# A QKV product on one core: casts and turns of the first rows placed between products, and another order of the last pair's products and stores

## Chip, cores, metric

One core of one Trainium2 chip. The metric is the device time of one execution in microseconds (us). The kernel before had a median of 362.59 us in three runs (362.5 to 362.67) when the prediction was made.

## The reference

```python
# x: (16, 512, 768) float32, w_qkv: (768, 2304) float32
qkv = np.matmul(x, w_qkv)
q, k, v = qkv[..., :768], qkv[..., 768:1536], qkv[..., 1536:]
return np.stack([q, k, v], axis=0)
```

## The kernel before

PE is the matmul engine, DVE the vector engine, ACT the scalar engine, POOL GpSimd, SP the sync engine. The 8192 rows of x are worked in 32 pairs of 128-row blocks. The 2304 columns are four blocks of 512 and a remainder of 256. The first three pairs ("rows 1 to 6") are multiplied in bf16 directly; from the fourth pair on, each pair makes two quads a and b, of seven products each (named 1 to 7), with sums of x and of the weights prepared by POOL and DVE. A "turn" is a transpose on PE. The parts that matter:

```python
def copy_halves(dst, src, two):            # one half on DVE, the other on ACT
    nc.vector.tensor_copy(out=dst[0], in_=src[0])
    if two: nc.scalar.activation(dst[1], src[1], ident)
    else:   nc.vector.tensor_copy(out=dst[1], in_=src[1])
def cast_rows(p, two=True): ...            # both rows of pair p: xc (bf16) <- xin (fp32)
def turn_rows(p, two=True): ...            # per row: 6 transposes into PSUM, copy_halves to xb
def busy(n): ...                           # n matmuls on zeros, to get PE's clock up
# ... loads, in order: x pair 0, x pair 1, six k-blocks of weights, remainder weights, x pair 2, ...
busy(11)
cast_rows(0); turn_rows(0)
busy(4)
cast_rows(1); cast_k(0); cast_k(1)         # cast_k(j): k-block j of the weights to bf16, on DVE
turn_rows(1)
for j in range(2, KT): cast_k(j)
# ... casts of the remainder's weights
block(0, 0, b1[0], singles, nothing)       # rows 1 to 4, k by k: 24 products
rem(0); rem(1)                             # remainder columns of rows 1 to 4
cast_rows(2, False); turn_rows(2, False)
block(0, 0, b1[0], halves((4, 5)), nothing)     # rows 5 and 6: 12 products
# ... then the block with weights bt ("the products of bt"), two more blocks, and 29 pairs

def last(a, b):                            # the last pair
    do(a,1); do(b,1); do(a,2); do(a,6); do(b,2); do(b,6)
    for u in (a, b): store_cols(u, 0, 0, CB, nc.sync)
    for u in (a, b): do(u,5); do(u,7); store_cols(u, 1, CB, 2*CB, nc.sync)
    do(a,4); store_cols(a, 1, 0, CB, nc.scalar); rem_stored(0)
    do(b,4); store_cols(b, 1, 0, CB, nc.scalar)
    for u in (a, b): do(u,3); store_cols(u, 0, CB, 2*CB, nc.sync)
    rem_stored(1)
```

`rem_stored(r)` multiplies one row's remainder columns, copies them out of PSUM on ACT and issues their store on ACT. c21 is what product 4 makes, c12 what product 3 adds to.

## Time and profile before

| | value | how to read it |
|---|---|---|
| time | 362.59 us (362.5 to 362.67) | three timed runs |
| the profiled run | 363.13 us, span 361.3 us | the run from which the trace comes; note that it is 0.5 us slower than any of the three timed ones |
| PE busy | 98% | the middle is bound by the number of matmuls |
| turns of rows 3 and 4 start | 8.51 us | PE had waited for them; first product (matmul of x with weights) at 9.30 |
| first product of bt | 20.65 us | where everything that the change does at the head is over |
| PE ends | 356.96 us | about 4.4 us of stores and closing follow |

A transfer "lands" when the trace records its completion. The profile's lines that carry this are in the prediction below.

### The profile page before, as it was taken

What the parts mean: (1) busy time and instruction counts of PE and PEld (TensorE: products, weight loads), DVE (VectorE), ACT (ScalarE), POOL (GpSimd) and SP (SyncE); (2) the same over time, 40 slices, a digit from 0 to 9 for tenths busy, and PEclk for the clock granted to TensorE, in tenths of its full rate; (3) what the DMA queues carried; (4) which work ended last, traced back from release to release, by engine and by line L of the source; (5) the groups of instructions that cost most, each with busy time, mean ns of one, the idle gap of its engine ahead of it and who ended that gap; (6) DMA issues with size and microseconds to landing.
All of it is one profiled execution on the core that took longest, in us unless ns stands there. A gap on an engine that the chain in (4) does not pass through costs nothing.

```text
span 361.3 us, 5221 instructions
## 1 busy us (share of the span) xinstructions
PE 353.4 (98%) x1765; PEld 251.0 (69%) x1797; DVE 224.4 (62%) x239; ACT 182.9 (51%) x304; POOL 173.9 (48%) x180
## 2 busy tenths in 40 slices
PE   8999999999999999999999999999999999999995
PEld 3644577777777777777777777777777777777763
DVE  3499826765566765566675565676556676556642
ACT  4547555455454545454545445455545454545452
POOL 0001861746664445664445665444665444666410
PEclk9999999999999999999999999999999999999999
DMA  7999869988898999899899999998989899999666
GB/s 298 405 388 373 286 221 359 331 289 295 278 328 301 294 273 294 276 324 315 280 280 290 281 308 309 291 289 278 292 288 321 295 300 271 297 272 339 264 261 232
DMA packets 80617, 108.08 MB, mean 299 GB/s; under 512 B 4816, under 2 KB 60368, under 8 KB 80592
## 3 DMA queue, kind: packets, MB, share of 16 engines
q1 hardware_dynamic: 65184, 96.35, 80.8%
q10 hardware_dynamic: 15408, 11.41, 9.6%
q8 instruction: 14, 0.23, 0.3%
q14 instruction: 11, 0.09, 0.1%
HBM read 32.24 MB, written 75.50 MB: 298 GB/s over the span
## 4 chain that ended last, share of the span: by engine, by line
PE 96%; ACT 1%; issue 1%; ACTq 0%; DVE 0%
PE ps L212 75%; PE ps L262 11%; PE ps L385 9%; PE ps L365 1%; PE ps L167 1%; ACT o L243 0%; ACTq L303 0%; ACT xb L147 0%; ACT orem L317 0%; DVE xb L145 0%; ACT xc L147 0%; ACTq L319 0%; DVE zero L346 0%; ACTq L317 0%
## 5 line engine op out<-in xcount | busy, mean ns | idle before, releaser
L212 PE MATMUL ps<-t,s 128*128 128x512 f32 x696 | 173.8, 398 | 0.0
L212 PEld LDWEIGHTS ps<-t,s 128*128 128x128 f32 x696 | 130.7, 188 | 29.7
L175 POOL CAST xb<-xf 128x1536 bf16<-128x1536 f32 x29 | 43.8, 1510 | 168.3 <-DVE xf L130 156.0
L240 DVE TENSOR_TENSOR o<-o,ps 128x512 f32<-128x512 f32 x58 | 39.9, 688 | 91.2 <-ACT o L239 91.2
L130 DVE STREAM_TRANSPOSE xf<-xin 128x1536 f32<-128x1536 f32 x29 | 85.5, 2950 | 3.7 <-DMA out_dram<-orem 2.1
L212 PE MATMUL ps<-b,xb 128*128 128x512 bf16 x320 | 82.4, 380 | 1.5
L239 ACT ACTIVATE o<-ps 128x512 f32<-128x512 f32 x58 | 34.8, 600 | 44.2 <-PE ps L212 44.2
L212 PEld LDWEIGHTS <-xb 128*128 128x128 bf16 x348 | 31.7, 98 | 35.6 <-issue 7.3
L233 ACT ACTIVATE o<-ps 128x512 f32<-128x512 f32 x58 | 34.9, 601 | 42.1 <-PE ps L212 39.4
L246 DVE TENSOR_TENSOR o<-o,ps 128x512 f32<-128x512 f32 x58 | 39.9, 688 | 21.3 <-PE ps L212 20.2
L212 PE MATMUL ps<-b,s 128*128 128x512 f32 x174 | 48.7, 389 | 0.0
L262 PE MATMUL ps<-w_rem,xb 128*128 128x256 bf16 x384 | 47.2, 273 | 0.0
L243 ACT ACTIVATE o<-ps 128x512 f32<-128x512 f32 x58 | 34.7, 599 | 24.1 <-PE ps L212 21.3
L226 ACT ACTIVATE o<-ps 128x512 f32<-128x512 f32 x58 | 34.7, 598 | 23.8 <-DVE o L246 20.6
L262 PEld LDWEIGHTS <-xb 128*128 128x128 bf16 x384 | 37.4, 98 | 11.2 <-issue 0.5
L230 DVE TENSOR_TENSOR o<-o,ps 128x512 f32<-128x512 f32 x58 | 36.5, 673 | 5.4 <-PE ps L212 4.1
L212 PEld LDWEIGHTS ps<-b,s 128*128 128x128 f32 x174 | 32.7, 188 | 6.8
L184 POOL TENSOR_TENSOR s<-s,xf 128x384 fp32r<-128x384 f32 x29 | 30.0, 1035 | 2.3
L183 POOL TENSOR_TENSOR s<-xf 128x384 fp32r<-128x384 f32 x29 | 30.9, 1064 | 0.0
L185 POOL TENSOR_TENSOR s<-xf 128x384 fp32r<-128x384 f32 x29 | 29.5, 1017 | 0.0
L187 POOL TENSOR_TENSOR s<-xf,s 128x384 fp32r<-128x384 f32 x29 | 29.5, 1016 | 0.0
L272 ACT ACTIVATE orem<-ps 128x512 f32<-128x512 f32 x31 | 18.5, 598 | 20.7 <-PE ps L262 19.5
(36 smaller groups left out, 129.4 us busy)
## 6 DMA issues: line engine op xcount, KB each, us to landing
out_dram<-o SPq DMA_DIRECT2D x62, 768.0 KB, 4.8
out_dram<-o SPq DMA_DIRECT2D x65, 256.0 KB, 4.1
xin<-in_x_dram SPq DMA_DIRECT2D x62, 192.0 KB, 6.9
xin<-in_x_dram ACTq DMA_DIRECT2D x54, 192.0 KB, 4.4
out_dram<-orem SPq DMA_DIRECT2D x31, 256.0 KB, 5.7
st<-in_w_qkv_dram SPq DMA_DIRECT2D x6, 768.0 KB, 13.1
xin<-in_x_dram SPq DMA_DIRECT2D x3, 768.0 KB, 5.7
st<-in_w_qkv_dram SPq DMA_DIRECT2D x6, 256.0 KB, 6.1
```

The source lines that it names most:

```text
L130: nc.vector.transpose(t[:].rearrange("p j (g b) -> p g j b", b=G), xin.pop(p)[:].rearrange("p g (a j) -> p g j a", a=G),)
L175: nc.gpsimd.tensor_copy(out=xb[p][:], in_=xf[p][:])
L212: nc.tensor.matmul(ps[:], lhs[j], rhs[j], start=(start and j == 0), stop=(j == KH - 1), skip_group_check=True,)
L226: nc.scalar.activation(c11, u.x[:], ident)
L230: nc.vector.tensor_tensor(c11, c11, u.z[:], op=add)
L233: nc.scalar.activation(c12, u.x[:], ident)
L239: nc.scalar.activation(c22, u.x[:], ident)
L240: nc.vector.tensor_tensor(c22, c22, u.y[:], op=add)
L243: nc.scalar.activation(c21, u.x[:], ident)
L246: nc.vector.tensor_tensor(c12, c12, u.y[:], op=add)
L262: nc.tensor.matmul(ps, xb[p][:, j, r * P:(r + 1) * P], w_rem[j // KH][:, j % KH, :], start=(j == 0), stop=(j == KT - 1), skip_group_check= ...
L385: nc.tensor.matmul(ps[n][:], xb[p][:, j, r * P:(r + 1) * P], w[:, j, :], start=(j == 0), stop=(j == KT - 1), skip_group_check=True,)
```

## The change

Its intent: at the head, rows 3 and 4 are cast and turned one at a time, between the first products of rows 1 and 2; rows 5 and 6 are cast and turned one at a time, each behind one remainder. At the tail, the last pair's stores are spread so that fewer bytes are left at the end, and the last product's columns are added and stored in two halves. The core of the diff:

```diff
-    busy(4)
-    cast_rows(1)
-    cast_k(0)
-    cast_k(1)
-    turn_rows(1)
+    busy(4)
+    cast_row(1, 0)
+    cast_k(0)
+    cast_row(1, 1)
+    cast_k(1)
+    def third_row():
+        turn_row(1, 0)
+        cast_k(2)
+    def fourth_row():
+        turn_row(1, 1)
+        for j in range(3, KT): cast_k(j)
     ...
-    block(0, 0, b1[0], singles, nothing)
-    rem(0)
-    rem(1)
-    cast_rows(2, False)
-    turn_rows(2, False)
-    block(0, 0, b1[0], halves((4, 5)), nothing)
+    block(0, 0, b1[0],
+        [((0, ), (0, 1)), third_row, ((1, ), (0, 1)), fourth_row, ((0, 1), (2, 3))]
+        + [((j, ), range(4)) for j in range(2, KT)], nothing)
+    for p in range(2):
+        rem(p)
+        cast_row(2, p, False)
+        turn_row(2, p, False)
+    block(0, 0, b1[0], [(range(KT), (4, )), (range(KT), (5, ))], nothing)
     ... in last(a, b), after products 1 and 2 and the stores of c11:
+        do(a, 6); do(a, 5); do(b, 6); do(a, 7)
+        store_cols(a, 1, CB, 2 * CB, nc.sync)
+        do(b, 5); do(b, 7)
+        store_cols(b, 1, CB, 2 * CB, nc.sync)
+        do(a, 4)
+        store_cols(a, 1, 0, CB, nc.sync)
+        do(a, 3)
+        store_cols(a, 0, CB, 2 * CB, nc.sync)
+        rem_stored(0)
+        rem_stored(1)
+        do(b, 4)
+        store_cols(b, 1, 0, CB, nc.sync)
+        product(b, 3, b.y, False)
+        for lo in (CB, CB + CB // 2):
+            hi = lo + CB // 2
+            part = b.o[:, 0, lo:hi]
+            nc.vector.tensor_tensor(part, part, b.y[:, lo - CB:hi - CB], op=add)
+            store_cols(b, 0, lo, hi, nc.scalar)
```

The remainder's weights are also loaded in two transfers instead of one.

More of the change, by code (lines that the diff above doesn't have):

```diff
@@ L151, with cast_row, turn_row @@
     xc = {}
-    def cast_rows(p, two=True):
-        src = xin.pop(p)
-        xc[p] = s_pool.tile([P, 2, K], bf16, name="xc", tag="s")
-        for r in range(2):
-            halves = (slice(0, K // 2), slice(K // 2, K))
-            copy_halves([xc[p][:, r, n] for n in halves], [src[:, r, n] for n in halves], two)
-    def turn_rows(p, two=True):
-        c = xc.pop(p)
-        xb[p] = xb_pool.tile([P, KT, 2 * P], bf16, name="xb", tag="xb")
-        for r in range(2):
-            cols = c[:, r, :].rearrange("m (p j) -> m j p", j=KT)
-            ps = ps_pool.tile([P, KT, P], bf16, name="ps")
-            for j in range(KT):
-                nc.tensor.transpose(ps[:, j, :], cols[:, j, :], eye)
-            ks = (slice(0, KH), slice(KH, KT))
-            copy_halves(
-                [xb[p][:, n, r * P:(r + 1) * P] for n in ks], [ps[:, n, :] for n in ks], two
-            )
+    def cast_row(p, r, two=True):
+        if r == 0:
+            xc[p] = s_pool.tile([P, 2, K], bf16, name="xc", tag="s")
+        halves = (slice(0, K // 2), slice(K // 2, K))
+        copy_halves([xc[p][:, r, n] for n in halves], [xin[p][:, r, n] for n in halves], two)
+    def turn_row(p, r, two=True):
+        if r == 0:
+            xb[p] = xb_pool.tile([P, KT, 2 * P], bf16, name="xb", tag="xb")
+        cols = xc[p][:, r, :].rearrange("m (p j) -> m j p", j=KT)
+        ps = ps_pool.tile([P, KT, P], bf16, name="ps")
+        for j in range(KT):
+            nc.tensor.transpose(ps[:, j, :], cols[:, j, :], eye)
+        ks = (slice(0, KH), slice(KH, KT))
+        copy_halves(
+            [xb[p][:, n, r * P:(r + 1) * P] for n in ks], [ps[:, n, :] for n in ks], two
+        )
     def round_x(p):
@@ L319, in rem_stored @@
             nc.scalar.dma_start(out_flat[1, row:row + P, R_OFF - H:R_OFF - H + REM], o[:, 0, :])
-        do(a, 1)
-        do(b, 1)
-        do(a, 2)
-        do(a, 6)
-        do(b, 2)
-        do(b, 6)
+        for n in (1, 2):
+            for u in (a, b):
+                do(u, n)
         for u in (a, b):
             store_cols(u, 0, 0, CB, nc.sync)
-        for u in (a, b):
-            do(u, 5)
-            do(u, 7)
-            store_cols(u, 1, CB, 2 * CB, nc.sync)
+        do(a, 6)
+        do(a, 5)
+        do(b, 6)
+        do(a, 7)
+        store_cols(a, 1, CB, 2 * CB, nc.sync)
+        do(b, 5)
+        do(b, 7)
+        store_cols(b, 1, CB, 2 * CB, nc.sync)
         do(a, 4)
-        store_cols(a, 1, 0, CB, nc.scalar)
+        store_cols(a, 1, 0, CB, nc.sync)
+        do(a, 3)
+        store_cols(a, 0, CB, 2 * CB, nc.sync)
         rem_stored(0)
+        rem_stored(1)
         do(b, 4)
-        store_cols(b, 1, 0, CB, nc.scalar)
-        for u in (a, b):
-            do(u, 3)
-            store_cols(u, 0, CB, 2 * CB, nc.sync)
-        rem_stored(1)
+        store_cols(b, 1, 0, CB, nc.sync)
[5 more added lines that the diff above has]
+            store_cols(b, 0, lo, hi, nc.scalar)
     NS = 3
@@ L349, with load_k @@
     make_identity(nc, eye)
+    st_0 = tq_pool.tile([P, KT, CB], fp32, name="st0", tag="tq")
+    stage[0, 0, 0], stage[0, 1, 0] = st_0[:, :KH, :], st_0[:, KH:, :]
+    def load_k(j):
+        load_w(st_0[:, j:j + 1], j, 1, Q_OFF[0], CB)
     load_rows(1)
-    load_blocks(0, 0, 1)
+    for j in range(KT):
+        load_k(j)
     st_rem = o_pool.tile([P, KT, REM], fp32, name="str", tag="o")
-    load_w(st_rem[:], 0, KT, R_OFF, REM)
+    for h in range(2):
+        load_w(st_rem[:, h * KH:(h + 1) * KH], h * KH, KH, R_OFF, REM)
     load_rows(2)
-    load_blocks(0, 1)
+    load_blocks(0, 1, KH)
     load_blocks(1, 0)
@@ L378, in block @@
         ps = {}
-        for js, tiles in groups:
+        for group in groups:
+            if callable(group):
+                group()
+                continue
+            js, tiles = group
             for n in tiles:
@@ L399, in halves @@
         return [(range(h * KH, (h + 1) * KH), tiles) for h in range(2)]
-    singles = [((0, ), (0, 1)), ((1, ), (0, 1)), ((0, 1), (2, 3))]
-    singles += [((j, ), range(4)) for j in range(2, KT)]
     act, dve = nc.scalar, nc.vector
-    def cast_k(j):
-        dve.tensor_copy(out=b1[0][:, j, :], in_=stage[0, j // KH, 0][:, j % KH, :])
     def cast_next(q, c, w):
@@ L416 @@
     busy(11)
-    cast_rows(0)
-    turn_rows(0)
+    cast_row(0, 0)
+    cast_row(0, 1)
+    turn_row(0, 0)
+    turn_row(0, 1)
     busy(4)
-    cast_rows(1)
+    cast_row(1, 0)
     cast_k(0)
+    cast_row(1, 1)
     cast_k(1)
-    turn_rows(1)
-    for j in range(2, KT):
-        cast_k(j)
-    act.activation(w_rem[1][:], st_rem[:, KH:], ident)
-    dve.tensor_copy(out=w_rem[0][:], in_=st_rem[:, :KH])
+    def third_row():
[3 more added lines that the diff above has]
+        turn_row(1, 1)
+        for j in range(3, KT):
+            cast_k(j)
+        dve.tensor_copy(out=w_rem[0][:], in_=st_rem[:, :KH])
+        act.activation(w_rem[1][:], st_rem[:, KH:], ident)
     bt0 = bt_pool.tile([P, KT, CB], bf16, name="bt")
     bt1 = bt_pool.tile([P, KT, CB], bf16, name="bt")
-    block(0, 0, b1[0], singles, nothing)
-    rem(0)
-    rem(1)
-    cast_rows(2, False)
-    turn_rows(2, False)
-    block(0, 0, b1[0], halves((4, 5)), nothing)
+    block(
+        0, 0, b1[0],
+        [((0, ), (0, 1)), third_row, ((1, ), (0, 1)), fourth_row, ((0, 1), (2, 3))]
+        + [((j, ), range(4)) for j in range(2, KT)],
+        nothing,
+    )
+    for p in range(2):
[3 more added lines that the diff above has]
+    block(0, 0, b1[0], [(range(KT), (4, )), (range(KT), (5, ))], nothing)
     for h in range(2):
```

## The prediction

> **What bounds the kernel now.** I read the page's first two parts first, then the chain of waits in order of time, then the stretches, and only then the timeline of the first 20 us and of the last 16 us, because the change touches nothing between them.
>
> ```profile
> PE 353.4 (98%) x1765; PEld 251.0 (69%) x1797; DVE 224.4 (62%) x239; ACT 182.9 (51%) x304; POOL 173.9 (48%) x180
> ...
> PEclk9999999999999999999999999999999999999999
> ```
>
> PE is busy 98% of a 361.3 us span at the full clock. The chain of waits says the same: 96% of it is PE, and each pair of quads in the steady part takes the same 10.74 us with no foreign link. So the middle is bound by the number of matmuls. The change leaves that number alone (2117 PE rows in both programs), so it can only win what PE does not have at the two ends. The stretches give their size:
>
> ```profile
> core 0: us, PE busy (x) PEld busy (x) DVE busy (x) ACT busy (x) POOL busy (x), PEclk, DMA share, GB/s
> 0.00:8.51 8.51, 6.79 (x28) 3.02 (x28) 2.61 (x9) 3.80 (x8) 0.71 (x6) 1.00 0.77 292
> 8.51:14.64 6.13, 6.08 (x37) 3.27 (x39) 2.93 (x8) 2.72 (x6) 0.00 (x0) 1.00 1.06 402
> 14.64:20.65 6.01, 5.84 (x48) 4.09 (x48) 4.19 (x11) 3.00 (x6) 0.00 (x0) 1.00 1.05 405
> ...
> 356.96:361.30 4.34, 0.00 (x1) 0.00 (x0) 0.06 (x1) 0.39 (x1) 0.00 (x0) 1.00 0.59 211
> ```
>
> Before 8.51 us PE mostly multiplies zeros to get warm; from there to 20.65 it lacks 0.2 us in all; after 356.96 it is done and 4.34 us of stores and closing follow. The chain through the first rows, in order of time:
>
> ```profile
> 7.13 0.91 ACT xb L147 x2
> 8.04 0.42 ACT xc L147
> 8.46 0.05 issue
> 8.51 0.95 PE ps L167 x12
> 9.46 2.16 PE ps L385 x10
> 11.62 0.05 issue
> 11.67 2.97 PE ps L385 x13
> 14.64 2.62 PE ps L262 x24
> 17.26 0.35 PE ps L167 x6
> 17.61 0.02 issue
> 17.63 0.37 DVE xb L145
> 18.00 0.05 issue
> 18.05 0.39 PE ps L385
> ```
>
> The reader sees two places where PE waits for another engine: until 8.51, for ScalarE's half of the cast of row 3 (xc), with the turned rows 1 and 2 (xb) ready since 8.04; and at 18.05, for VectorE's first copy out of the turn of row 5. The last links are the closing stores:
>
> ```profile
> 355.53 0.61 ACT o L243
> ...
> 356.53 0.44 ACTq L303
> ...
> 357.08 0.39 ACT orem L317
> ```
>
> The transfer issued after that link, at 357.49, is the last of all: in the trace's record of landings it comes at 359.87, and the end of the span 1.43 us later.
>
> **What the Trainium skill says.** "TensorE: Matmul & The Clock Gate", section "Wait — 56ns, not 53.3ns?", gives 215.7 ns from start to start for warm 512-column matmuls; here 24 of them go from 9.46 to 14.64, 0.2158 us each: agreed. The same page, section "What's actually happening", has a cold array run at half rate until some 3.4 us of activity: the 11 matmuls on zeros start 0.43 us apart until about 5 us, and the next four take 1.03 us together, so the array is warm before real work starts and PE idling half a microsecond less changes no clock. "VectorE: DVE Perf Modes", section "The TRN2 errata", gives (N+151)/0.96 ns for an fp32 add; the 512-column adds on o take 688 to 689 ns against 691: agreed. I use it for the new 256-column adds, of which this trace has none. "DMA: Bandwidth & Descriptors", section "Anatomy of one DMA", says most of a transfer's fixed cost of about 2 us is the receipt at its end (fitted for transfers from GpSimd). The 128 KB stores here take 1.9 to 2.2 us from issue to landing, against about 0.33 us of moving at the 404 GB/s seen from 358 to 359: agreed in size.
>
> **The change, first part: the head.** Casts, turns and products are as many as before. The weight load of the remainder columns becomes two transfers of half the size, which adds one issue of about 0.5 us on SyncE. The next load, x of the third pair, now waits for the first k-block's landing at 7.56 instead of x of the second pair at 6.92. It costs nothing, since the transfer engines run at 402 GB/s with a backlog: what was issued before is about 3.8 MB, of which 1.07 MB had moved by 5 us, so they are occupied until about 11.9 us anyway.
>
> What moves is the order. VectorE now does xc of row 3, the first k-block, xc of row 4, the second k-block. On the timeline the first of the xc casts starts at 7.43 and the second 0.27 later; so the first k-block's cast (0.42) runs 7.70 to 8.12, having landed at 7.56. PE may then multiply rows 1 and 2 by it at about 8.17, where it waited until 8.51 before. From there:
>
> - two products, 0.43: to 8.60. ScalarE's half of row 3 was ready at 8.46.
> - six turns of row 3, half of 0.95: to 9.07. The second k-block is cast by 8.73.
> - two products: to 9.50; six turns of row 4: to 9.98, its cast being ready at about 8.9.
> - two products of row 3: to 10.41. Row 4's copy out of PSUM starts 0.1 after its turns and takes 0.37: PE waits until about 10.5.
> - two products of row 4 and the 16 left of this block, 18 x 0.2158 = 3.88: to 14.38.
>
> Before, that point was 14.64. Gain **0.26**: 0.34 from the earlier start, less 0.08 for the copy of row 4. The next stretch has the same 24 remainder matmuls (2.62) and 12 turns (about 0.7) in both kernels. Before, PE stood 0.1 for the copy of row 5 (turns over about 17.96, products at 18.05). In the new order row 5 is turned between the two remainders, its copy lies beside the second of them, and the first six products use row 5 alone while row 6 is copied. That gains **0.1**, if the casts of row 5 (x landed 14.72, first cast 14.85, two casts to 15.5) are ready at 15.68, and those of row 6 (behind row 5's copies, about 17.3) at 17.37. Both margins are thin, so I count 0.08. Sum for the head: **0.34**. It reaches the end only if nothing downstream is tied to absolute time. Each pair starts without a wait now; the fourth pair's sums on GpSimd end at 43.99 with its first products of that kind at 48.98, and the sixth pair's transpose, which waits for x, ends at 62.0 with its products due at about 66.7. So I carry it over whole.
>
> **Second part: the tail.** PE has the same 30 fp32, 12 bf16 and 12 remainder matmuls, all back to back (busy 10.98 of 10.98), and every product that reuses a bank has at least one other between it and its reader, so PE ends issuing at 356.80 in both. Before, a remainder row was last: PE, ScalarE 0.39, issue at 357.49, landing 359.87, behind about 0.9 MB still moving after 357. After, the last product is quad b's third. The lag from the start of the last matmul to the VectorE add was 0.43 (355.21 to 355.64), so the first half-add starts at about 357.0; each takes (256+151)/0.96 = 424 ns, an estimate; the second half is ready at 357.85 and issued on ScalarE's queue at 357.87. Ahead of it, quad a's last columns leave at about 355.0 instead of 356.4, both remainders by 356.1, and b's c21 at about 357.05 and 357.45. The backlog is then gone and the last 128 KB needs the unloaded 1.7 to 1.9 us (the store at 352.89 landed in 1.69): landing 359.6 to 359.8. Gain **0.1 to 0.25**, central 0.15. The last issue is 0.38 us later than before; the lighter queue pays for it. Cutting the add in two buys about 0.27 us against one add of 0.69.
>
> Sum: 0.34 + 0.15 = 0.49, so 362.59 - 0.49 = **362.1 us**.
>
> **Rivals.** (1) The head gains nothing, because the wait moves: PE in the new order waits for a k-block cast or the copy of row 4 where it waited for the cast of row 3. For it: VectorE is in order and its copies now wait for PE's turns, with k-block casts behind them. Against it: the k-blocks land 0.6 to 0.7 us apart ahead of use, the last at 10.85. The time would be 362.4. (2) The tail gets longer: the last issue is later, and if a 128 KB store takes the 2.2 us that the remainder stores take, it lands at 360.1, 0.2 later than now. Against it: fewer bytes are queued before it. With the head's gain the time would be 362.45. (3) The tail gains more, because the stores left after PE ends are 512 KB against nearly twice that and the end is set by the drain: up to 0.5 less at the end, 361.7. Against it: the fixed receipt time cannot be drained away. (4) The head's gain is swallowed later by loads tied to the transfer engines (their share is 0.99 from 20 to 44 us): 362.45.
>
> **Range and chances.** Head 0.0 to 0.5 and tail -0.2 to 0.5 are hardly likely to meet at their ends; eight times in ten the sum should lie between 0.1 and 1.0: **361.6 to 362.5 us**. Two per cent is 7.25 us; all of PE's idle time and the closing stores together are less than 8 us, so faster by over 2% has 0.01, slower 0.01, within 2% 0.98.
>
> **What would show it right or wrong.** Right: the first real product at about 8.2 instead of behind twelve turns; the steady pairs still 10.74 us apart and 0.3 to 0.4 earlier throughout; PE ending with an fp32 product; two adds of about 0.42 us; last landing 2.6 to 2.8 us after PE's last issue instead of 3.07. Wrong: a wait of PE on VectorE's copies of more than 0.15 us before 20 us, a pair starting late for its sums or its x, or closing stores that are still queued when the last one is issued.

## The result, and the profile after

| | before | after |
|---|---|---|
| median | 362.58 us (362.5 to 363.3, 6 runs) | 362.76 us (362.67 to 362.82, 6 runs) |
| profiled run, span | 363.13 us, 361.3 us | 362.72 us, 360.9 us |

The ratio is 1.0002, with a 95% interval of 0.9989 to 1.0015: the same. A ratio is the mean time of one kernel's fast runs over that of the other's in the same rounds, so it is not quite the ratio of the medians. The measured 362.76 lies above the predicted range (361.6 to 362.5).

The table's two rows contradict each other at first sight: the profiled run of after is 0.4 us quicker than that of before, the timed runs are not. The chain of waits of the kernel after, in order of time (start, length, what):

```profile
6.70 0.69 DVE xb L145 x2
7.39 0.27 DVE xc L145
7.66 0.34 DVE b L423
...
8.05 0.59 PE ps L402 x2
...
10.20 4.06 PE ps L402 x18
14.25 1.31 PE ps L260 x12
15.56 0.41 PE ps L165 x6
15.97 1.31 PE ps L260 x12
17.28 0.48 PE ps L165 x6
17.76 25.90 PE ps L402 x120
```

The link to ACT's cast of row 3 is gone, as intended; the first product comes at 8.05 behind DVE's cast of the first k-block (L423). The first product of bt starts at 20.19 instead of 20.65, and all the pairs follow 0.46 us earlier, still 10.74 us apart. So against that one trace the head gained 0.46 us, more than the 0.34 predicted.

The end of the kernel after, from its timeline (start, length, engine, line):

```profile
355.39 0.38 ACT L315 ACTIVATE orem<-ps 128x256 f32<-128x256 f32 x1 [0.51 <-PE ps L260]
...
355.80 0.37 ACTq L317 DMA_DIRECT2D out_dram<-orem  x1
356.22 0.60 ACT L241 ACTIVATE o<-ps 128x512 f32<-128x512 f32 x1 [0.45 <-PE ps L210]
356.56 0.75 DVE L344 TENSOR_TENSOR o<-o,ps 128x256 f32<-128x256 f32 x2 [2.04 <-PE ps L210]
357.01 0.82 ACTq L301 DMA_DIRECT2D out_dram<-o  x2
```

The half-adds are there (0.75 for both). The copy of b's c21 out of PSUM (L241) starts at 356.22; the 0.45 idle before it are put down to PE, but the line above shows what ACT was doing until 356.17: issuing the second remainder's store. By the trace's record of landings, the last four 128 KB stores land at 358.55, 358.89, 359.23 and 359.56, about 0.34 apart: a train.

### The profile page after: what moved, and what is told of

Same layout as the page of the kernel before. It is cut to its first block, busy times and chain, and to the rows that moved or that the text cites. A ratio compares the mean times of both kernels' runs of the same rounds, so it can differ in the third digit from the quotient of the medians.

```text
span 360.9 us, 5256 instructions
## 1 busy us (share of the span) xinstructions
PE 355.1 (98%) x1797; PEld 250.8 (69%) x1797; DVE 224.4 (62%) x240; ACT 182.5 (51%) x304; POOL 173.5 (48%) x180
## 4 chain that ended last, share of the span: by engine, by line
PE 98%; DVE 1%; DVEq 0%; issue 0%
PE ps L210 76%; PE ps L260 12%; PE ps L402 9%; PE ps L377 1%; PE ps L165 1%; DVE xb L145 0%; DVE o L344 0%; DVE b L423 0%; DVEq L520 0%; DVE zero L350 0%; DVE xc L145 0%
## 5 line engine op out<-in xcount | busy, mean ns | idle before, releaser
L210 PE MATMUL ps<-b,xb 128*128 128x512 bf16 x348 | 84.7, 380 | 0.0
L241 ACT ACTIVATE o<-ps 128x512 f32<-128x512 f32 x58 | 34.7, 598 | 24.1 <-PE ps L210 21.8
```

The lines of the kernel that those rows point to most:

```text
L210: nc.tensor.matmul(ps[:], lhs[j], rhs[j], start=(start and j == 0), stop=(j == KH - 1), skip_group_check=True,)
L241: nc.scalar.activation(c21, u.x[:], ident)
```

## The experiments

All runs told here are of the fast state; "quick" and "slow" below mean the two ends of the spread within it. Every run is the same as the kernel before within 2%: the ratios go from 0.9980 to 1.0023, so most of the argument rests on places in the traces. The rounds ran on different chips, each with the kernel before beside it. Each traced run can be cut into three parts: the first product of bt; from there to the first fp32 product of the pairs, 28.33 us in every one of these traces; and from there to the end of the span, "the tail" below. For the head two more numbers are needed: when PE's full clock was granted (the trace's clock record), and when the twelfth turn, the last of rows 1 and 2, starts.

### before_again, after_again, head_only, tail_only

The first two are the unchanged kernels. The profiled run of before had been slower than all of its timed runs, so the trace itself was under suspicion. The others are halves of the change:

```diff
 head_only: the kernel after, with last(a, b) as before
 tail_only: the kernel before, with last(a, b) as after
```

> The unchanged kernel before, to get a second trace of it. Its first trace came from a run of 363.13 us, while its timed runs have a median of 362.58. Theory A: that trace shows an unusual run, 0.5 us slow in one stage; a new trace has a span of about 360.8 instead of 361.3, and the place of the 0.5 us shows where the two traces part (the head is suspected: the first turns ran at half clock until 6.74 us). Rival B: the trace is usual and the 0.5 us come from outside the span: the new trace again has 361.3 and the same starts of each stage. Timed: 362.6 either way, ratio 1.000.

> The unchanged kernel after. Theory A: 362.75 us, ratio 1.0003 to 1.0005 to the kernel before, trace with a span of 360.9 to 361.0 as the first. Rival B: the same time, so this run alone does not tell; it gives the size of the difference (0.1 to 0.2 us) with its interval and the spread of the traces.

> The new order of the first rows with the old last pair. Prediction's head term (0.34 gained): 362.2 us. Theory A (the wait that the new order removes is not there in a usual run, so the head gains nothing): 362.5 to 362.65. Rival C (the head gains 0.34 and the tail loses 0.5): 362.2.

> The old order of the first rows with the new last pair. Prediction's tail term (0.15 gained): 362.4 us. Theory A: the tail costs 0.1 to 0.2: 362.7 to 362.8 (in the traces the last landing came 3.07 us after the last matmul's start before and 3.44 after). Rival C: 363.1.

Measured (before in the same rounds: 362.83, 362.53 to 363.31, 9 runs):

| run | median, range (5 runs) | profiled run | clock granted at | twelfth turn | first product | bt | tail |
|---|---|---|---|---|---|---|---|
| (before, the first trace) | | 363.13 | 6.74 | 6.90 | 9.30 | 20.65 | 312.37 |
| before_again | 362.54, 362.50 to 363.20 | 362.54 | 5.30 | 6.29 | 8.69 | 20.04 | 312.39 |
| tail_only | 362.90, 362.64 to 363.40 | 363.40 | 7.17 | 7.03 | 9.49 | 20.84 | 312.41 |
| (after, the first trace) | | 362.72 | 6.49 | 6.78 | 8.05 | 20.19 | 312.39 |
| after_again | 362.72, 362.69 to 362.80 | 362.69 | 6.16 | 6.62 | 7.94 | 20.17 | 312.38 |
| head_only | 362.68, 362.60 to 362.87 | 362.64 | 3.91 | 6.31 | 7.96 | 20.20 | 312.31 |

Three things follow. First, the trace that the prediction was read from is one of a slow run: another run of the same kernel has bt 0.61 us earlier. Second, the slow place is the head. In the old order bt comes 13.74, 13.75 and 13.82 us after the twelfth turn: what delays the first turns delays everything, one for one. In the new order bt hardly moves (20.17 to 20.20) while the turn moves by 0.47; only when the turn comes later still does bt follow (tail_whole below: turn at 7.03, bt at 20.41). Third, the old tail (312.31 to 312.39) and the new one (312.38 to 312.41) are the same to within 0.1: the predicted gain of 0.15 is not there.

The turns themselves, from the PE timelines, first of the kernel before (first trace), then of before_again:

```profile
5.86 1.26 PE L167 MATMUL ps<-eye,xc 128*128 128x128 bf16 x12
```

```profile
5.59 0.93 PE L167 MATMUL ps<-eye,xc 128*128 128x128 bf16 x12
```

With the clock granted at 6.74 they start 0.27 later, because the eleventh product on zeros is still running, and take 0.33 longer; together they make up the 0.61 us between the two runs. The landing of the first x, which also varies from run to run, does not explain it: it came at 4.89 in the slow trace and at 4.96 in the quick one. The chain of before_again:

```profile
6.53 0.90 ACT xb L147 x2
7.43 0.42 ACT xc L147
...
7.90 0.95 PE ps L167 x12
```

The turns of rows 3 and 4 start at 7.90 here, not at 8.51. In the new order the first product takes that place on PE, and it cannot come earlier: the first k-block lands at 7.46 (head_only), its cast takes 0.43, and the first product follows at 7.96. The chain of head_only says so itself, it goes through the transfer:

```profile
1.73 5.73 DMA st<-in_w_qkv_dram
...
7.48 0.44 DVE b L417
...
7.96 0.59 PE ps L396 x2
```

### tail_sp, tail_whole

```diff
 tail_sp: the kernel after
-            nc.scalar.dma_start(out_flat[1, ...], o[:, 0, :])          # in rem_stored(r)
+            (nc.scalar, nc.sync)[r].dma_start(out_flat[1, ...], o[:, 0, :])
 tail_whole: the kernel after
-        for lo in (CB, CB + CB // 2):
-            hi = lo + CB // 2
+        for lo in (CB, ):
+            hi = lo + CB
```

> The kernel after, with the second remainder row's store issued on SyncE instead of ScalarE. Theory T1 (in the new tail ScalarE issues that store for 0.37 us just when quad b's c21 should leave PSUM, and the four last 128 KB stores then form a train 0.34 us apart that starts late): the c21 copy starts 0.37 earlier (now 356.22 in the trace), the last landing comes 0.25 to 0.35 earlier, 362.4 us against 362.7. Rival T2 (the tail is set by the half-adds and the receipt of the last store alone): no change, 362.7.

> The kernel after, with the last add in one piece of 512 columns and one 256 KB store. T1 (the train of stores sets the end, the split is hidden behind it): 0.00 to 0.1 slower, 362.7 to 362.8. T2 (the last add and the last store's own latency set the end, as the prediction had it): 0.27 slower or more, 363.0.

Measured: tail_sp 362.67 us (362.64 to 362.79), tail 312.30. tail_whole 362.99 us (362.91 to 363.15), tail 312.57, against 312.38 to 312.39 of after (before in these rounds: 362.84).

tail_sp, timeline of the end:

```profile
355.88 0.33 SPq L317 DMA_DIRECT2D out_dram<-orem  x1
355.94 0.60 ACT L241 ACTIVATE o<-ps 128x512 f32<-128x512 f32 x1
356.57 1.04 SPq L301 DMA_DIRECT2D out_dram<-o  x2
```

With the store issued on SP, the copy of c21 starts at 355.94, and its idle note is gone. Allowing for PE's end, 0.08 later in this run, that is 0.36 earlier, as T1 expected. The last landing gained only 0.15 (310.89 against 311.04 us after the first fp32 product), half of the expectation. The trace shows one reason: the second piece of c21 was issued at 357.27, just after the first remainder's store landed at 357.26, whose completion semaphore it uses again. The split of the last add is not settled by tail_whole. Its median is 0.27 above that of after, the figure of T2, but its profiled run had a late clock (7.12) and reached bt 0.23 later, which is the head and not the tail. Its tail alone is longer by 0.19, and of that only 0.06 is in the last landing (311.10 against 311.04 after the first fp32 product); the rest comes after it, in SP's closing waits (three were left then instead of one; they are told of below). The landing is within what T1 allowed (0.00 to 0.1), the median is not.

### fill_copy, fill_old_second

```diff
 fill_copy: the kernel after
-    fourth_row, ((0, 1), (2, 3))] + [((j, ), range(4)) for j in range(2, KT)]
+    fourth_row, ((0, 1), (2, )), ((2, ), (0, 1)), ((0, 1), (3, )), ((2, ), (2, 3))]
+    + [((j, ), range(4)) for j in range(3, KT)]
 fill_old_second: fill_copy, and
-    for p in range(2):
-        rem(p); cast_row(2, p, False); turn_row(2, p, False)
-    block(0, 0, b1[0], [(range(KT), (4, )), (range(KT), (5, ))], nothing)
+    for p in range(2): rem(p)
+    for r in range(2): cast_row(2, r, False)
+    for r in range(2): turn_row(2, r, False)
+    block(0, 0, b1[0], halves((4, 5)), nothing)
```

> The kernel after, with the products of rows 1 and 2 by the third k-block placed between row 3's and row 4's first products, so that PE has work while row 4 is copied out of PSUM. The wait there is 0.18 us in three traces (predicted 0.08). If it is on the path: 0.15 to 0.2 faster, 362.55. Rival (the landing of x for rows 5 and 6 at 14.6 us holds the next stage anyway): 362.7, the 0.18 comes back as a wait before the turns of row 5.

> The variant that fills row 4's copy wait, with the old order of rows 5 and 6 (both remainders, then casts, then turns). Theory H (in the new order row 5 is turned one remainder earlier and so waits for its x, landed at 14.6 to 14.7, and its casts; every gain of the first block is lost there): the products of bt start 6.17 after the remainders instead of 6.4, at 20.1, 0.15 to 0.2 earlier than with the new order: 362.55. Rival (something else holds bt near 20.2): 362.75.

Measured: fill_copy 362.78 us (362.69 to 362.82; before in its rounds 362.84), no gain over after; fill_old_second 362.50 us (362.48 to 362.63; before in its rounds 362.70). In fill_copy the remainders start at 13.91 and bt at 20.31, 6.39 later; in fill_old_second at 13.96 and 20.13, 6.17 later. The PE timeline of fill_copy shows where the 0.1 us that it had won at the remainders went:

```profile
13.91 1.47 PE L260 MATMUL ps<-w_rem,xb 128*128 128x256 bf16 x12
15.55 0.54 PE L165 MATMUL ps<-eye,xc 128*128 128x128 bf16 x6 [0.16 <-DVE xc L149]
15.92 1.47 PE L260 MATMUL ps<-w_rem,xb 128*128 128x256 bf16 x12
```

and its DVE timeline what its casts had waited for:

```profile
14.86 0.36 DVE L145 CAST xc<-xin 128x384 bf16<-128x384 f32 x1 [2.41 <-DMA xin<-in_x_dram]
```

So theory H holds: turning row 5 one remainder earlier ties PE to the landing of x for rows 5 and 6 (14.73 in this run). In the old order the second remainder covers that landing.

### nine_zeros, late_zeros_before, late_zeros_after

These ask whether the clock's grant is the cause of the spread, or only goes with it.

```diff
 nine_zeros: the kernel before
-    busy(11)
+    busy(9)
 late_zeros_before, late_zeros_after: the kernels before and after
-    nc.vector.memset(zero[:], 0.0)
+    for _ in range(7):
+        nc.vector.memset(zero[:], 0.0)
-    busy(11)   ...   busy(4)
+    busy(6)    ...   busy(2)
```

> The kernel before, with 9 multiplications of zeros ahead of the first turns instead of 11. Theory A (the time of before depends on when the full clock is granted in that run, because at half clock the 11 zeros hold the first turns until 5.86 us where row casts are ready at 5.56, and the turns then run at half rate): the quick runs stay at 362.5, the slow ones come down by up to 0.28 us, none over 363.1, median 362.5 to 362.7. Rival B (the spread of before has another source): the same spread to 363.3.

> The kernel before with the zeros starting later: seven fillings of the zero tile instead of one (some 1.6 us), 6 products on it instead of 11 and 2 instead of 4, so that they still end at about 5.5 us. Theory A (the grant of the full clock comes after PE has been busy for a while, at a point that differs from run to run; the first turns at half clock end 0.5 us later and the old order passes that on one for one): the grant is never before 6.5 us, all runs are slow: none below 362.8, median 363.0 to 363.3. Rival B (the spread of before has another source, the grant only goes with it): the same mixture as before, with runs at 362.5.

> The same edit to the kernel after. Theory A: the new order passes on only what goes beyond the first k-block's landing: first product at the end of the turns plus 1.22, 8.1 to 8.35; median 362.75 to 362.95, at least 0.2 below late_zeros_before. Rival B: 362.7 as without the edit, with no difference to late_zeros_before beyond that of the unedited pair. If the grant comes after 8.5 us in some runs, products run at half clock there and both lose up to 0.5 more.

nine_zeros gave 362.99 us (362.52 to 363.30), a miss: the slow runs did not come below 363.1. Its trace (clock at 6.55, twelfth turn 6.76, bt 20.51, that is 13.75 after the turn) keeps to the old order's rule. Its x landed late (5.16), so the first turn started at 5.76, and most of the turns ran at half rate all the same; fewer zeros do not help that. The spread is the one that Rival B had forecast: as the two were written down, this result favours B, and only the trace is in theory A's favour.

The late zeros say more:

| run | median, range (5 runs) | clock granted at | twelfth turn | first product | bt |
|---|---|---|---|---|---|
| late_zeros_before | 363.58, 363.55 to 363.72 | 7.72 | 7.24 | 9.73 | 21.08 |
| late_zeros_after | 363.19, 362.80 to 363.47 | 9.25 | 7.24 | 8.61 | 20.98 |

Before, in the same rounds, unedited: 362.63 (362.49 to 363.34, 9 runs). The turns of late_zeros_before, all at half rate:

```profile
6.07 1.49 PE L167 MATMUL ps<-eye,xc 128*128 128x128 bf16 x12
```

When the grant is put off on purpose, the quick runs vanish altogether and the old order is at 363.55 at best, more than the 363.0 to 363.3 that were expected (the first zeros started at 3.53, later than planned, and the first turn at 6.07). The new order loses less, by 0.39 us in the medians, also as expected, though its median is above the 362.75 to 362.95 named; in its trace the grant came at 9.25, after the first products had begun, which run at half rate until then. So a late grant costs the old order what slow runs lose, and the new order less. Not all of the 363.58 is the grant's: the edit also puts the first turn at 6.07, 0.21 later than in any trace with the usual zeros. That the grant is what spreads the ordinary runs rests on this and on their traces together. Why it comes when it does in an ordinary run, anywhere from 3.84 to 7.17 us in fourteen traces with eleven or nine zeros from 1.19 on, no experiment here explains.

### rows_last, best, best_loads

```diff
 rows_last: the kernel after, end of last(a, b)
-        rem_stored(0); rem_stored(1)
         do(b, 4); store_cols(b, 1, 0, CB, nc.sync)
+        rem_stored(0)
         product(b, 3, b.y, False)
         ... the two half-adds, their stores on nc.sync instead of nc.scalar
+        rem_stored(1)
 best: rows_last, the filled order of fill_copy, and for rows 5 and 6
+    for r in range(2): cast_row(2, r, False)
+    rem(0)
+    rem(1, lambda: turn_row(2, 0, False))       # turned between the two rows of rem(1)
+    turn_row(2, 1, False)
+    block(0, 0, b1[0], [(range(KT), (4, )), (range(KT), (5, ))], nothing)
 best_loads: best, with k-block 0 loaded and cast ahead of pair 1, busy(2) for busy(4),
            row 4 turned straight after row 3, and k-block 2 cast after both
```

> The kernel after with another order of the last products: a4 a3 b4 remainder b3 remainder, b's halves on SyncE. Theory T1 (the end is set by when the last four stores can start and by their train of 0.34 us each, so the large ones must be ready earlier and a single 128 KB last): last landing 0.5 to 0.75 earlier after the first fp32 product of the pairs (310.3 to 310.5 us instead of 311.04), 362.0 to 362.2. Rival T2 (the drain is bound by bytes whatever their order): 362.55 to 362.7.

> The filled wait, rows 5 and 6 cast ahead and turned between the single rows of the second remainder, and the tail of rows_last. If the parts add: bt at 19.85 (0.35 earlier than after), and the tail's 0.5 to 0.75: 361.6 to 361.9. If an absolute time downstream (weights for the next blocks, x for the fourth pair) holds it: no more than rows_last.

> The same with the first k-block of the weights loaded ahead of the second pair's x and two zero products fewer. Theory (in the new head the first products wait for the first k-block, landed at 7.45 to 7.55): it lands at 5.6, first products at 7.0, bt 0.4 to 0.6 earlier than in best, 361.2 to 361.4. Rival (the second pair's x, 0.65 later, takes its place): as best.

| run | median, range (5 runs) | ratio to before, interval | bt | tail |
|---|---|---|---|---|
| rows_last | 362.32, 362.24 to 362.43 | 0.9991 (0.9977 to 1.0004) | 20.19 | 312.00 |
| best | 361.87, 361.82 to 362.21 | 0.9980 (0.9968 to 0.9993) | 20.03, clock at 7.03 | 312.00 |
| best_loads | 362.43, 362.36 to 362.83 | 0.9996 (0.9984 to 1.0009) | 20.32 | 311.99 |

rows_last gained 0.38 us on the tail of after, short of the 0.5 to 0.75 expected: its last nine stores land about 0.34 us apart, without a gap from 356.43 to 359.18, so by this trace what is left there is bytes. Of its two changes, the order of the products and the queue of b's halves, neither was run alone. best is the only version whose interval lies below 1 against the kernel before, and beats both kernels (0.2%, still the same within 2%). It lies in the range expected, though its bt of 20.03 is not the 19.85 of that sum: it comes in a run with a late clock (7.03), where the kernel after has 20.41 (tail_whole, clock at 7.12). Its PE timeline has no idle note left at rows 5 and 6:

```profile
16.11 0.50 PE L165 MATMUL ps<-eye,xc 128*128 128x128 bf16 x6
16.45 0.82 PE L260 MATMUL ps<-w_rem,xb 128*128 128x256 bf16 x6
17.10 0.50 PE L165 MATMUL ps<-eye,xc 128*128 128x128 bf16 x6
```

best_loads was a miss. Its first product came at 6.83, but x of rows 3 and 4 landed at 8.22 instead of 6.8 to 6.9, and everything behind it some 0.7 later, more than the one k-block put ahead of it takes (0.65 between landings): the turns of row 3 started at 8.82 and bt at 20.32.

## Why the prediction was wrong

**The step that failed: "Gain 0.26: 0.34 from the earlier start, less 0.08 for the copy of row 4".** Its working was read from the trace, and the trace was of a run of 363.13 us, while the same result listed three runs at 362.5 to 362.67. The subtraction was then made from 362.59. In a run with an early clock the old order starts its turns of rows 3 and 4 at 7.90 and reaches bt at 20.04 (before_again, the only such trace of it); the new one has its first product at 7.94 to 8.04, 0.50 to 0.51 after the landing of the first k-block, and reaches bt at 20.17 to 20.28 (after_again, head_only, tail_sp). There the new head loses 0.13 or more. In runs with a late clock it gains 0.46 (20.65 against 20.19), or 0.43 where the twelfth turn comes at 7.03 in both (20.84 of tail_only against 20.41 of tail_whole): more than the 0.34 predicted. So in quick runs the change had nothing to gain: PE waits for ScalarE's cast there too, but only until 7.90, and the landing of the first k-block keeps the new order from starting before 7.94. A mean over runs is near nothing: over all 47 timed runs of the kernel before it is 362.75 us (362.45 to 363.37), over 11 of the kernel after 362.74 us (362.67 to 362.82). What the head's change bought is a narrower spread, not a shorter mean.

**The sentence behind it: "the array is warm before real work starts and PE idling half a microsecond less changes no clock".** The prediction placed the end of the half clock at about 5 us, by the spacing of the products on zeros; in that trace all eleven start 0.43 apart, the last at 5.43. The first turns are real work, and in that trace they too ran at half rate, until 6.74: their 1.26 us for twelve stood in the timeline, beside 0.95 for the next twelve. late_zeros_before shows the size of what this moves.

**The head's second term, 0.08 gained at rows 5 and 6.** Its margins were called thin, and they were: in the runs with an early clock the turn of row 5 waits for its casts. Between the remainders' start and bt, after needed 6.10 and after_again 6.19, before 6.17; fill_copy 6.39. So 0.07 of it was there in the first trace of after, and a loss in the others. The first rival, the wait that moves, had been named for row 4's copy and the k-blocks; the runs put it mainly at the first k-block's landing and at x of row 5. Row 4's copy cost 0.18, not 0.08, above the 0.15 that the prediction had named as a sign of being wrong (in head_only row 3's second product starts at 9.71 and row 4's first at 10.11, where 0.22 would do).

**The tail's term, 0.15 gained; measured 0.0 to 0.1 lost** (312.38 to 312.41 against 312.31 to 312.39). The issue of the last store came where it was predicted (357.44; predicted 357.87 less the 0.44 that PE ended earlier), the landing did not: 2.11 us later and not 1.7 to 1.9, because c21's pieces were still ahead of it (they landed at 358.55 and 359.23; in tail_sp, with c21 issued earlier, the last store took 1.94). They were late by 0.23 against the prediction (first issue 356.84 against 357.05 less 0.44), as ACT was issuing the remainder's store when c21 was ready; tail_sp shows that much. The last landing therefore comes 0.14 later after the pairs' start than before (311.04 against 310.89 to 310.91). The span gave this back: SP ends by waiting for its completion semaphores in a fixed order, about 0.06 us for each; before, three waits were left when the last store landed and the span ended 1.48 us later, after, one was left and it was 1.35. The second rival, a longer tail, was half right, and so was the other sign of being wrong: closing stores were still queued when the last one was issued.

**Sums and readings that do not hold.** The sign for the tail, 2.6 to 2.8 us from PE's last issue to the last landing, does not follow from the prediction's own figures (359.6 to 359.8 less 356.80 is 2.8 to 3.0); it measured 3.44 (356.12 to 359.56). The span before ends 1.48 us after the last landing, not 1.43, as it is 361.35 long. The 128 KB stores of the old end take 1.69 to 2.37 us, not 1.9 to 2.2. The "2117 PE rows" are in no view: both pages list 1797 weight loads, so the point that they are equal stands.

**What was right:** that it is the same within 2%; that the middle passes the head's shift on whole (28.33 us and 10.74 us per pair throughout); the first product near 8.2 in a run with a late clock (8.05); half-adds of 0.42 us. Set against runs with a late clock, the head's gain had the right mechanism and nearly the right size (0.46, 0.34 predicted); the time of 362.59 from which it was subtracted was that of quick runs.

## What to carry to other kernels

Compare the time of the profiled run with the timed runs before reading a trace to a tenth of a microsecond: what a wait seen in one trace is worth may hold only in the slower part of the runs. When a wait for one engine is taken away, ask first what else lands at that moment; here a load that landed 0.14 us before its use in the prediction's own working was the next bound. And an engine that also issues transfers is busy while it does so: its name in a wait should be looked up in its queue's lines as well.

## What the Trainium skill lacked or had wrong

- "TensorE: Matmul & The Clock Gate", section "What you observe": the page has the change of clock at around 4 us of activity, give or take 0.5 us. Here the grant came 3.84 to 7.17 us into the span with products from 1.19 on, so 2.65 to 5.98 us after the first, over fourteen traces. In the order before that is worth up to 0.8 us (bt at 20.04 to 20.84), 0.2% of the time, which agrees with the "<1%" of the page's section "What's actually happening".
- "VectorE: DVE Perf Modes", section "The TRN2 errata": the page checks its formula (N+151)/0.96 at 512 and 2048 columns. For 256 columns an estimate by it is 424 ns, and the two half-adds took 421 and 411 ns, within about 3% of it. The second started before the first had ended: both together took 0.75 us, not 0.84.
- "DMA: Bandwidth & Descriptors", section "Issuing engines are not separate DMA queues", calls the time that a sequencer spends on issuing usually small relative to the transfer. That is so here (0.37 us against 2.02 from issue to landing). The section does not say that the issuing engine's own next work waits that long: ACT's copy of c21, for which the end waited, started at 356.22 instead of 355.86.
- None of the pages used tells of a train of closing stores such as this one: 128 KB stores land about 0.34 us apart, whether the last two are issued on ACT (after) or on SP and ACT in turn (rows_last). From 358 to 359 us of after, while they land, the transfer engines are busy throughout and move 379 GB/s.
